# Zero products ahead of the first transposes, a fixed order on three engines, and a first scale column in two parts, in a two-layer trunk on one Trainium2 core

## The chip, the core and the metric

The kernel runs on one core of a Trainium2 chip. Five engines work side by side, each through its own queue in order: TensorE (PE; the profile lists its weight loads apart as PEld) multiplies matrices into PSUM banks, VectorE (DVE) and ScalarE (ACT) do elementwise work and read the banks, GpSimd (POOL) fills tiles and issues some transfers, and SyncE (SP) issues most of the transfers. The metric is the device time of one execution in microseconds, as the median of several runs. Lower is better.

## What is computed

A chunk of 512 tokens of width 1024 goes through two layers. Each layer has a token mixer and a feed-forward part, and each of these is wrapped in the same frame: a norm, a scale and a shift that come from a conditioning vector `c`, the mixer itself, a second norm and a gate. The first mixer is an attention without softmax.

```python
def rms_norm(x, g):
    xf = x.astype(jnp.float32)
    y = xf * lax.rsqrt(jnp.mean(xf * xf, axis=-1, keepdims=True) + EPS)
    return (y * g.astype(jnp.float32)).astype(x.dtype)

def ada_modulation(c, w, b):
    m = jax.nn.silu(c) @ w + b
    shift, scale, gate = jnp.split(m, 3, axis=-1)
    return shift[:, None, :], scale[:, None, :], gate[:, None, :]

def reference(x, c, ...):
    for i in range(DEPTH):
        shift, scale, gate = ada_modulation(c, mix_ada_w[i], mix_ada_b[i])
        h = rms_norm(x, mix_pre_g[i]) * (1.0 + scale) + shift
        if i % N_MIXERS == 0:
            y = stick_breaking_mixer(h, sb_w_qkv[j], sb_w_o[j])
        else:
            y = token_mixing_mixer(h, tm_w_in[j], ...)
        x = x + gate * rms_norm(y, mix_post_g[i])
        ...
        y = swiglu(h, ffn_w_gate[i], ffn_w_up[i], ffn_w_down[i])
        x = x + gate * rms_norm(y, ffn_post_g[i])
    return x
```

This text is about the very beginning: the first `rms_norm`, the first `scale` and `shift`, and the first projection `h @ w_qkv`.

## The kernel before

Tokens are taken in four tiles of 128 (`tt` 0 to 3), the width of 1024 in eight blocks of 128 (`k` 0 to 7). A product of two float32 matrices is made from three products of parts (`mm3`): each operand is split into a high part (ACT, `wh`, `hTh`) and the rest (DVE, `wl`, `hTl`).

The first stage works as follows.

- `norm0(tt)` squares a tile of x on ACT (into `junk`, with the sum in `sx`), takes the root on ACT (`sd`), the reciprocal on DVE (`r`), and scales the tile on DVE.
- `turn0(tt)` turns the tile with eight transposes on PE into two PSUM banks (`tp`). Four copies then bring it into `xhT`, which holds x with the width on the partitions. Before the change ACT makes two of them and DVE two for tiles 0 and 1; ACT makes all four for tiles 2 and 3.
- `row0(raws)` multiplies silu(c), one column (`sc`), with a block of the modulation weights (`ada`): eight products of 1 by 256 in float32, four for each of two weight tiles, into one bank. The result (`row`) is copied by DVE and set upright by two small products with `oneb`. `row0(a0)` gives scale and shift of block k = 0, `row0(a1)` those of k = 1. Those of the other blocks are summed by DVE (`ada0_sum`, with `acc`), set upright by `sums0`, and started by `cols0`.
- `h0` applies scale and shift to a block of `xhT` on ACT, twice: once rounded (`hTh`), once in full; DVE forms the difference `hTl`.
- `v_step` and `qk0_step` multiply block after block with the weights of v (`v`), q (`pq`) and k (`pk`), 512 columns at a time. When all eight blocks are through, the second half of v follows (`v1` in the code), and the attention starts beside it.

Weights come through `wget` and `wemit` in a fixed stream: SP loads a 512 KB tile (`raw`), ACT forms `wh`, DVE forms `wl`. There are two `raw` tiles, so the third load waits until `wl` of the first is made. The weights of the modulation have eight tiles of their own (`ra`) in a pool that is closed after the stage; tiles called `ones`, which POOL fills and SP completes, then take that memory. `G`, the gate of the first mixer, is summed by DVE from `rawada` tiles in eight steps.

The order of each engine's queue is chosen by a scheduler at build time from the code's order and its own estimates. Three switches override it: while `pe["chain"]`, `dve.chain` or `act.chain` is set, each new instruction that goes through the wrapper of that engine is bound to stand behind the last one. Before the change none of them is set in the first stage; PE's is set where the attention starts, so from there PE's queue is written out in the code. `bank` gives PSUM banks in turn: six under one tag, two under the tag "p".

Of the kernel before, what the change touches and what calls it, by code (L numbers as in the profile page):

```python
# [8 lines left out]
F32 = mybir.dt.float32  # L9
F32R = mybir.dt.float32r  # L10
AF = mybir.ActivationFunctionType
ALU = mybir.AluOpType

P = 128
# [21 lines left out]
def trunk(ctx: ExitStack, tc: tile.TileContext, A: dict, out: bass.AP):  # L36
# [17 lines left out]
    def nm(s):  # L54
        uid[0] += 1
        return f"{s}_{uid[0]}"

    def slot(dt, name, a=2, b=512):
        return s4.tile([P, a, b], dt, tag="s4", name=nm(name))

    def bank(name, tag="b"):
        return psum.tile([P, 512], F32, tag=tag, bufs=6 if tag == "b" else 2, name=nm(name))

    pe = {"prev": None, "chain": False}

    class Vector:


        chain, prev = False, None
# [11 lines left out]
    dve = Vector()  # L81

    class Scalar:


        chain, prev = False, None
# [8 lines left out]
    act = Scalar()  # L95

    def pe_op(b):

        if pe["chain"] and pe["prev"] is not None:
            order(b, pe["prev"])  # L100
        pe["prev"] = b

    def order(b, before):
        tc.add_manual_dep(
            b.ins, before.ins.name,
            mybir.DependencyInfo(mybir.DependencyClass.NoSync, mybir.DependencyReason.DATA),
            reason="order",
        )

    def mm(o, l, r, start, stop, after=None):  # L110
        b = nc.tensor.matmul(o, l, r, start=start, stop=stop, skip_group_check=True)  # L111
        pe_op(b)
        if after is not None:
            order(b, after)
# [3 lines left out]
    def transpose(o, i):  # L118
        last_tp[0] = nc.tensor.transpose(o, i, ident)  # L119
        pe_op(last_tp[0])  # L120
# [21 lines left out]
    last_low = [None]  # L142
    last_block, summed, normed = [None], [None], [None]

    raws = []
# [11 lines left out]
    def wemit():  # L157
        n = len(got)
        src, a, b, key = stream[n]
        if len(raws) == n:  # L160
            wload()
        if key[0] == "vblocks":
            got.append(vblocks(raws[n]))
            return
        if src is None:
            if key[1][0] != "u" and (not first_blocks or n > first_blocks[-1] + KF):
                first_blocks.append(n)
            for _ in blocks(*next_raws(n)):
                pass
            return  # L170
        raw = raws[n]
        if key[0] == "wdn" and key[2] in SEVEN[key[1]]:
            got.append(down_blocks(raw))
            return
        h, l = wtile(a, b, SHORT if key[0] in ("wgu", "win_u") else 16)
        if key[0] == "wqk" and key[1]:

            act.activation(h[:], raw[:], AF.Copy)
            nc.vector.tensor_tensor(l[:], raw[:], h[:].bitcast(F32), ALU.subtract)
            if len(raws) == n + 1 and stream[n + 1][3][0] == "wqk":  # L180
                wload()
        else:
            high = act.activation(h[:], raw[:], AF.Copy)
            last_low[0] = nc.vector.tensor_tensor(l[:], raw[:], h[:].bitcast(F32), ALU.subtract)  # L184
            if edge[0] and key[0] == "wgu":
                order(high, feature[1])
                order(last_low[0], feature[0])
        got.append((h, l))
# [154 lines left out]
    def wget(src, look=3):  # L343

        n = taken[0]
        taken[0] += 1
        while len(got) < min(n + 1 + look, len(stream)):
            wemit()
        assert stream[n][3] == src, (stream[n][3], src)
        return got[n]  # L350
# [44 lines left out]
    stp = st0.__enter__()  # L395

    def ada0_raw(b, q):

        nk, n = (4, 256) if b < 2 else (2, 512)
        raw = stp.tile([P, nk, n], F32, tag="ra", bufs=8, name=nm("ada0"))  # L400
        load(raw[:], A["ada0s"][b, q] if b < 2 else A["ada0p"][b - 2, q])
        return raw
# [3 lines left out]
    x0, a0 = [], []  # L406
    for tt in range(NT):
        xt = slot(F32, "x0", 1, 1024)
# [104 lines left out]
    def rms(part, first=None):  # L513

        bias = epsb
        if first is not None:
            bias = small.tile([P, 1], F32, tag="ss", name=nm("ss"))
            dve.tensor_scalar(bias[:], first, 1.0 / D, EPS, ALU.mult, ALU.add)
        sd = small.tile([P, 1], F32, tag="sd", name=nm("sd"))
        last_sqrt[0] = act.activation(sd[:], part, AF.Sqrt, bias=bias[:], scale=1.0 / D)  # L520
        r = small.tile([P, 1], F32, tag="r", name=nm("r"))
        return sd, r
# [201 lines left out]
    def norm0(tt):  # L724
        xt = x0[tt]
        junk = npool.tile([P, D], F32, tag="n", name=nm("junk"))
        sx = small.tile([P, 1], F32, tag="sx", name=nm("sx"))
        act.activation(junk[:], xt, AF.Square, accum_out=sx[:])
        sd, r1 = rms(sx[:])
        dve.reciprocal(r1[:], sd[:])  # L730
        dve.tensor_scalar(xt, xt, r1[:, 0:1], None, ALU.mult)

    def turn0(tt):
        xt = x0[tt]
        for q in range(2):
            ps = bank("tp0")
            for k in range(4):
                kk = q * 4 + k
                transpose(ps[:, k * P : (k + 1) * P], xt[:, kk * P : (kk + 1) * P])
            for k2 in range(2):  # L740
                dst = xhT[q * 2 + k2][:, :, tt * P : (tt + 1) * P]
                src = ps[:, k2 * 256 : (k2 + 1) * 256].rearrange("p (a b) -> p a b", a=2)
                if q and tt < 2:
                    dve.tensor_copy(dst, src)
                else:
                    act.activation(dst, src, AF.Copy)
# [47 lines left out]
    def cols0(k):  # L794

        ps = bank("ab0", "p")
        mm(ps[:, 0:4], ident, add[:, k : k + 2, :].rearrange("p n a -> p (n a)"), True, False)
        return ps
# [8 lines left out]
        )  # L807
        return ab

    def row0(raws):  # L810

        ps = bank("ab0", "p")
        for q, raw in enumerate(raws):
            for k in range(4):
                mm(ps[0:1, :256], sc[:, q * 4 + k : q * 4 + k + 1], raw[:, k, :], q + k == 0, q * 4 + k == 7)
        row = stp.tile([P, 256], F32, tag="row", bufs=2, name=nm("row"))
        dve.tensor_copy(row[0:1, :], ps[0:1, :256])
        ps = bank("ab0", "p")
        for i in range(2):
            mm(ps[:, i : i + 1], row[0:1, i * P : (i + 1) * P], oneb[0:1, 0:1], True, True)  # L820
        return ps
# [16 lines left out]
    wv0, wqk0 = [], []  # L838

    def qk0_step(k):  # L840
        for w, pb in zip(wqk0, (pq0, pk0)):
            h, l = hTk(hT, k, 0, T)
            mm3(pb[:], w[0][:, k, :], w[1][:, k, :], h, l, k == 0, k == KD - 1)

    norm0(0)
    norm0(1)
    turn0(0)
    norm0(2)
    ab0 = row0(a0)
    turn0(1)  # L850
    norm0(3)
    turn0(2)
    turn0(3)
    wv0.append(wget(("wv", 0, 0), 0))
    a2 = [ada0_raw(2, q) for q in range(4)]
    h0(scales(ab0, 0), 0, 0)
    ab1 = row0(a1)
    wqk0.append(wget(("wqk", 0, 0), 0))
    vb = [bank("v0") for _ in range(NT)]
# [6 lines left out]
    for b in range(1, 4):  # L866

        ps = cols0(2 * b)
# [34 lines left out]
    with tc.tile_pool(name="att", bufs=1) as att, tc.tile_pool(name="att2", bufs=2) as att2:  # L903
# [60 lines left out]
        for js in (B31, B2, B0):  # L964
            at, n = {}, 0
# [131 lines left out]
        zb = [bank("z") for _ in range(2)]  # L1097
        bg.bank = lambda: zb[0]
        cur = attend(0)
        for k in range(KD):  # L1100
            if k % 2 == 0:
                wv = wget(("wv", 1, k // 2))
# [7 lines left out]
            if k > 3:  # L1110
                tt = TURNS[k - 4]
# [693 lines left out]
```

## Time and profile before

| what | value |
|---|---|
| median of 3 runs | 1103.92 us (1100.98, 1103.92, 1109.13) |
| the profiled execution's own time | 1103.49 us |
| its span in the profile | 1101.7 us |
| DVE busy, ACT busy, POOL busy over the span | 88%, 55%, 3% |
| bytes read from memory, mean rate | 164.69 MB, 157 GB/s |
| first stage until the first v product | 0 to 22.94 us |
| v, q and k products over all blocks | 22.94 to 61.59 us |

The span is what the profile covers, from the first to the last instruction; the execution's own time has 1.8 us around it. All times below are microseconds from the start of the span. A row of the timeline gives start, duration, engine, line, operation, the tile written and the tiles read, partitions and elements, and how many equal instructions in a row it stands for. In brackets stands how long the engine was idle before, and what ended that.

A float32 product is run as two instructions: `row0` makes eight products, and the timeline counts sixteen. A row's duration on PE contains the time that a product needs to pass through the array, so the starts of successive rows, not their durations, give the pace.

### The profile page before, as it was taken

How to read it: one execution, taken by the hardware profiler on the slowest of the kernel's cores; microseconds unless marked ns; L12 is line 12 of the kernel's file. 1: busy time of each engine (PE TensorE's matmuls, PEld its weight loads, DVE VectorE, ACT ScalarE, POOL GpSimd, SP SyncE). 2: the span in 40 equal slices, each digit the busy share in tenths (PEclk: the TensorE clock that was granted, in tenths of full speed). 3: DMA queues.
4: the chain of work that ended last, by engine and by line, in shares of the span. 5: the costliest groups of instructions: out<-in, count | busy, mean ns of one | idle time of the engine just before them, and what ended most of it. 6: DMA issues, size and time to landing. Idle time of an engine off the chain costs nothing.

```text
span 1101.7 us, 18701 instructions
## 1 busy us (share of the span) xinstructions
PE 1082.1 (98%) x7452; PEld 978.7 (89%) x7452; DVE 972.8 (88%) x1293; ACT 610.1 (55%) x1016; POOL 29.5 (3%) x53
## 2 busy tenths in 40 slices
PE   7999999999999999999999999999999999999997
PEld 4787788788999999998888899988999999999996
DVE  4988999866989999989978999868979999899996
ACT  6554665665655555554252767526545555565662
POOL 0020100000000000001000000001000000000000
PEclk9999999999999999999999999999999999999999
DMA  8976434304433434359878324524334342332252
GB/s 317 357 226 218 138 121 131 122 17 153 153 111 124 163 124 153 134 187 347 294 246 322 143 87 137 177 95 163 122 113 153 136 159 100 107 113 96 77 190 78
DMA packets 51355, 176.38 MB, mean 160 GB/s; under 512 B 6074, under 2 KB 9146, under 8 KB 51268
## 3 DMA queue, kind: packets, MB, share of 16 engines
q1 hardware_dynamic: 48708, 166.81, 43.8%
q0 software_dynamic: 2560, 8.39, 2.1%
q8 instruction: 58, 0.95, 0.3%
q14 instruction: 29, 0.24, 0.1%
HBM read 164.69 MB, written 8.39 MB: 157 GB/s over the span
## 4 chain that ended last, share of the span: by engine, by line
PE 85%; DVE 7%; DMA 4%; issue 2%; ACT 2%; SPq 0%; DVEq 0%; ACTq 0%
PE r L111 35%; PE y L111 16%; PE pqk L111 7%; PE X L111 4%; PE gu L111 4%; PE Y L111 3%; PE v L111 3%; PE u L111 2%; PE av L111 2%; PE z L111 2%; PE tw L119 1%; PE Z L111 1%; PE W L111 1%; PE tp L119 1%; DVE wl L184 1%
## 5 line engine op out<-in xcount | busy, mean ns | idle before, releaser
L111 PE MATMUL r<-Sh,wh 128*128 128x256 f32 x640 | 177.3, 277 | 0.6 <-ACT e L89 0.6
L111 PE MATMUL r<-Sl,wh 128*128 128x256 f32 x640 | 177.0, 277 | 0.0
L111 PE MATMUL r<-Sh,wl 128*128 128x256 f32 x640 | 176.9, 277 | 0.0
L89 ACT ACTIVATE wh<-raw 128x1024 fp32r<-128x1024 f32 (+1 forms) x105 | 108.3, 1036 | 101.7 <-DMA raw<-in_wdown 36.1
L111 PE MATMUL y<-wh,as 128*128 128x512 f32 x480 | 150.5, 391 | 0.3 <-DVE svt L73 0.3
L111 PEld LDWEIGHTS r<-Sh,wh 128*128 128x128 f32 x640 | 120.2, 188 | 1.2 <-ACT e L89 1.0
L111 PEld LDWEIGHTS r<-Sl,wh 128*128 128x128 f32 x640 | 120.2, 188 | 0.1
L111 PEld LDWEIGHTS r<-Sh,wl 128*128 128x128 f32 x640 | 120.1, 188 | 0.0
L184 DVE TENSOR_TENSOR wl<-raw,wh 128x1024 fp32r<-128x1024 f32 x79 | 95.9, 1220 | 25.9 <-ACT wh L89 25.7
L73 DVE TENSOR_TENSOR wl<-f,wh 128x1024 fp32r<-128x1024 f32 x95 | 112.9, 1219 | 1.1 <-ACT wh L89 1.1
L89 ACT ACTIVATE wh<-f 128x1024 fp32r<-128x1024 f32 x95 | 100.2, 1055 | 17.3 <-DVE f L73 12.5
L111 PEld LDWEIGHTS y<-wh,as 128*128 128x128 f32 x480 | 90.0, 188 | 19.3 <-issue 0.6
L89 ACT ACTIVATE e<-r 128x256 f32<-128x256 f32 x120 | 45.9, 384 | 102.3 <-PE r L111 100.2
L111 PE MATMUL y<-wl,as 128*128 128x512 f32 x240 | 93.7, 391 | 0.0
L111 PE MATMUL r<-hTh,wh 128*128 128x256 f32 x320 | 88.8, 278 | 0.2 <-DVE gu L73 0.2
L111 PE MATMUL r<-hTh,wl 128*128 128x256 f32 x320 | 88.5, 277 | 0.0
L111 PE MATMUL r<-hTl,wh 128*128 128x256 f32 x320 | 88.5, 277 | 0.0
L111 PEld LDWEIGHTS r<-hTh,wh 128*128 128x128 f32 x320 | 60.1, 188 | 1.1 <-DVE gu L73 0.9
L111 PE MATMUL r<-hTh,b 128*128 128x256 f32 x320 | 60.9, 277 | 0.0
L111 PEld LDWEIGHTS r<-hTl,wh 128*128 128x128 f32 x320 | 60.1, 188 | 0.0
L111 PEld LDWEIGHTS r<-hTh,wl 128*128 128x128 f32 x320 | 60.1, 188 | 0.0
L89 ACT ACTIVATE wh<-rawx 128x1024 fp32r<-128x1024 f32 x40 | 42.5, 1062 | 29.7 <-PE r L111 28.9
(288 smaller groups left out, 2924.3 us busy)
## 6 DMA issues: line engine op xcount, KB each, us to landing
rawada<-in_ada SPq DMA_DIRECT2D x80, 512.0 KB, 6.3
rawy<-in_wy SPq DMA_DIRECT2D x38, 512.0 KB, 4.2
rawx<-in_wx SPq DMA_DIRECT2D x38, 512.0 KB, 3.4
raw<-in_wdown SPq DMA_DIRECT2D x22, 512.0 KB, 5.3
raw<-in_wdn SPq DMA_DIRECT2D x22, 512.0 KB, 3.4
raw<-in_wqk SPq DMA_DIRECT2D x16, 512.0 KB, 4.0
ada<-in_ada0p SPq DMA_DIRECT2D x12, 512.0 KB, 7.6
raw<-in_wgu SPq DMA_DIRECT2D x12, 512.0 KB, 3.5
```

Source lines behind the costliest of these rows:

```text
L73: b = getattr(nc.vector, op)(*args, **kw)
L89: b = nc.scalar.activation(*args, **kw)
L111: b = nc.tensor.matmul(o, l, r, start=start, stop=stop, skip_group_check=True)
L119: last_tp[0] = nc.tensor.transpose(o, i, ident)
L184: last_low[0] = nc.vector.tensor_tensor(l[:], raw[:], h[:].bitcast(F32), ALU.subtract)
```

## The change

`zero` is a tile of 128 by 256 zeros, filled by DVE, and `spin(n)` lets PE multiply it with itself n times into a bank `zb` that nobody reads. Twenty such products stand ahead of the first transposes, six between those of tile 0 and tile 1. `norm0` is split, so that the root, the reciprocal and the scaling (`root`) can stand behind the copies of an earlier tile. `turn0` takes both banks first and returns the copies as a function; ACT now copies the first bank and DVE the second for every tile. `row0(a0)` makes its first four products, then calls `between`, which holds the transposes and copies of tile 3 and the split of the first weight of v, and then makes the other four. Throughout, the order is bound on PE, DVE and ACT.

```diff
         act.activation(junk[:], xt, AF.Square, accum_out=sx[:])
-        sd, r1 = rms(sx[:])
-        dve.reciprocal(r1[:], sd[:])
-        dve.tensor_scalar(xt, xt, r1[:, 0:1], None, ALU.mult)
+
+        def root():
+            sd, r1 = rms(sx[:])
+            dve.reciprocal(r1[:], sd[:])
+            dve.tensor_scalar(xt, xt, r1[:, 0:1], None, ALU.mult)
+
+        return root
 
     def turn0(tt):
         xt = x0[tt]
+        tps = [bank("tp0") for q in range(2)]
         for q in range(2):
-            ps = bank("tp0")
             for k in range(4):
                 kk = q * 4 + k
-                transpose(ps[:, k * P : (k + 1) * P], xt[:, kk * P : (kk + 1) * P])
+                transpose(tps[q][:, k * P : (k + 1) * P], xt[:, kk * P : (kk + 1) * P])
+        return lambda: copies0(tt, tps)
+
+    def copies0(tt, tps):
+        for q, ps in enumerate(tps):
...
-                if q and tt < 2:
+                if q:
                     dve.tensor_copy(dst, src)
                 else:
                     act.activation(dst, src, AF.Copy)
...
-    def row0(raws):
+    zero = stp.tile([P, 256], F32, name="zero")
+    dve.memset(zero[:], 0.0)
+    zb = bank("zb")
+
+    def spin(n):
+
+        for _ in range(n):
+            mm(zb[:, 0:256], zero[:, 0:P], zero[:], True, True)
+
+    def row0(raws, between=None):
 
         ps = bank("ab0", "p")
         for q, raw in enumerate(raws):
+            if q and between is not None:
+                between()
             for k in range(4):
...
-    norm0(0)
-    norm0(1)
-    turn0(0)
-    norm0(2)
-    ab0 = row0(a0)
-    turn0(1)
-    norm0(3)
-    turn0(2)
-    turn0(3)
-    wv0.append(wget(("wv", 0, 0), 0))
+    pe["chain"] = dve.chain = act.chain = True
+    norm0(0)()
+    root = norm0(1)
+    spin(20)
+    turned = turn0(0)
+    root()
+    spin(6)
+    for tt in (2, 3):
+        root = norm0(tt)
+        turned()
+        turned = turn0(tt - 1)
+        root()
+    turned()
+
+    def between():
+        turn0(3)()
+        wv0.append(wget(("wv", 0, 0), 0))
+        order(last_low[0], dve.prev)
+
+    ab0 = row0(a0, between)
+    pe["chain"] = dve.chain = act.chain = False
```

In the rows of the order below, a name carries a running number, and `x_1` to `x_4` are the token tiles 0 to 3. First PE from its first product to the first v product, before:

```order
L119 MATMUL tp_39_164<-identt,x_1_89 128x128 x4
L119 MATMUL tp_40_171<-identt,x_1_89 128x128 x4
L119 MATMUL tp_48_200<-identt,x_2_95 128x128 x4
L119 MATMUL tp_49_207<-identt,x_2_95 128x128 x4
L111 MATMUL ab_45_186<-ada_5_101,sc 1x256 x4
L111 MATMUL ab_45_186<-ada_6_103,sc 1x256 x4
L119 MATMUL tp_54_222<-identt,x_3_97 128x128 x4
L111 MATMUL ab_47_197<-oneb,row_195 128x1 x2
L119 MATMUL tp_57_243<-identt,x_4_99 128x128 x4
L111 MATMUL ab_65_268<-ada_8_107,sc 1x256 x4
L111 MATMUL v_70_286<-wh_250,hTh_132 128x512
```

The same stretch of PE after the change:

```order
L111 MATMUL zb_150<-zero 128x256 x20
L119 MATMUL tp_38_182<-identt,x_1_89 128x128 x4
L111 MATMUL zb_150<-zero 128x256 x6
L119 MATMUL tp_44_210<-identt,x_2_95 128x128 x4
L119 MATMUL tp_50_232<-identt,x_3_97 128x128 x4
L111 MATMUL ab_54_251<-ada_5_101,sc 1x256 x4
L119 MATMUL tp_55_256<-identt,x_4_99 128x128 x4
L119 MATMUL tp_56_257<-identt,x_4_99 128x128 x4
L111 MATMUL ab_54_251<-ada_6_103,sc 1x256 x4
L111 MATMUL ab_60_280<-oneb,row_278 128x1 x2
L111 MATMUL ab_66_297<-ada_8_107,sc 1x256 x4
L111 MATMUL v_71_315<-wh_270,hTh_132 128x512
```

The zero products stand ahead of the first transposes and again ahead of those of tile 1; the products of the first scale column now end behind the transposes of tile 3, and the two small products (`oneb`) behind them, where before they stood ahead of most of tile 2's and all of tile 3's.

Now DVE, from the scaling of tile 3 (`x_4`) to the first scale and shift (`ab`), before:

```order
L73 TENSOR_SCALAR x_4_99<-x_4_99,r_219 128x1024
L73 COPY row_195<-ab_45_186 1x256
L184 TENSOR_TENSOR wl_251<-raw_105,wh_250 128x1024
L73 TENSOR_TENSOR ab_262<-ab_47_197,add 128x2
L73 TENSOR_TENSOR ab_262<-ab_262,mul 128x2
L73 TENSOR_TENSOR hTl_133<-xhT_128,hTh_132 128x512
L184 TENSOR_TENSOR wl_283<-raw_111,wh_282 128x1024
```

And DVE after the change:

```order
L73 TENSOR_SCALAR x_4_99<-x_4_99,r_244 128x1024
L73 COPY xhT_130<-tp_51_233 128x2x128
L73 COPY xhT_130<-tp_56_257 128x2x128
L184 TENSOR_TENSOR wl_271<-raw_105,wh_270 128x1024
L73 COPY row_278<-ab_54_251 1x256
L184 TENSOR_TENSOR wl_312<-raw_111,wh_311 128x1024
L73 TENSOR_TENSOR ab_291<-ab_60_280,add 128x2
L73 SCALAR_TENSOR_TENSOR acc_347<-ada_61_283,sc,acc_347 128x512
L73 TENSOR_TENSOR ab_291<-ab_291,mul 128x2
```

The copy of `row` moved behind the first `wl`, and the scale and shift moved behind the second `wl` and one step of a sum.

Last SP's queue at the end of the v, q and k products, around the tiles called `ones` and the loads for the gate, before:

```order
L128 DMA G_458<-in_adab 1x1024
L128 DMA cc<-in_consts 128x128
L128 DMA raw_640<-in_wv 128x1024
L128 DMA rawada_527<-in_ada 128x1024
L128 DMA rawada_575<-in_ada 128x1024
L128 DMA ones_607<-in_consts 128x128 x4
L128 DMA raw_646<-in_wv 128x1024
```

And after the change:

```order
L128 DMA cc<-in_consts 128x128
L128 DMA raw_669<-in_wv 128x1024
L128 DMA G_487<-in_adab 1x1024
L128 DMA ones_636<-in_consts 128x128 x3
L128 DMA rawada_556<-in_ada 128x1024
L128 DMA rawada_604<-in_ada 128x1024
L128 DMA raw_675<-in_wv 128x1024
```

Three loads of `ones` now stand ahead of the last five `rawada` loads, where they stood behind them. No queue differs in its order from the middle of the attention on.

## The prediction

> **What bounds the kernel now.** I read the page first, then the windows of the first stage, then its timeline row by row, since the change touches nothing behind it.
>
> ```profile
> PE 1082.1 (98%) x7452; PEld 978.7 (89%) x7452; DVE 972.8 (88%) x1293; ACT 610.1 (55%) x1016; POOL 29.5 (3%) x53
> ...
> PE 85%; DVE 7%; DMA 4%; issue 2%; ACT 2%; SPq 0%; DVEq 0%; ACTq 0%
> ```
>
> PE is busy for 98% of the span and carries 85% of the chain that ended last. So a time that is added to PE in the first stage should reach the end, unless a later wait takes it up. The windows show where that could happen (columns: stretch, length, busy time and count of PE, PEld, DVE, ACT, POOL, granted clock, DMA share, GB/s).
>
> ```profile
> 7.31:12.00 4.69, 3.95 (x17) 3.22 (x18) 2.50 (x6) 4.46 (x12) 0.00 (x0) 1.00 0.98 394
> ...
> 17.00:23.00 6.00, 6.00 (x37) 3.36 (x36) 2.48 (x6) 4.87 (x11) 0.00 (x0) 1.00 0.99 405
> 23.00:60.00 37.00, 36.38 (x172) 29.42 (x172) 35.64 (x48) 16.95 (x23) 4.84 (x10) 1.00 0.81 300
> ```
>
> From 23 to 60 us PE is busy for 36.38 of 37.00 us and DVE for 35.64: both are nearly full. The granted clock is 1.00 in each window, but the pace of the products is not the same, as the timeline of the start shows:
>
> ```profile
> 0.90 0.07 DVE L73 MEMSET mul<- 128x8 f32 x1
> ...
> 6.50 0.75 DVE L73 TENSOR_SCALAR x<-x,r 128x1024 f32<-128x1024 f32 x1
> ...
> 7.31 1.97 PE L119 MATMUL tp<-identt,x 128*128 128x128 f32 x8 [7.31 <-DVE x L73]
> ...
> 10.02 1.97 PE L119 MATMUL tp<-identt,x 128*128 128x128 f32 x8 [0.74 <-DVE x L73]
> ...
> 11.92 4.96 PE L111 MATMUL ab<-ada,sc 128*1 128x256 f32 x16
> ...
> 12.30 0.12 PEld L111 LDWEIGHTS ab<-ada,sc 128*1 128x1 f32 x1 [0.30 <-issue]
> ...
> 13.87 1.06 ACT L89 ACTIVATE wh<-raw 128x1024 fp32r<-128x1024 f32 x1
> ...
> 14.43 0.13 PEld L111 LDWEIGHTS ab<-ada,sc 128*1 128x1 f32 x1 [0.30 <-issue]
> 14.78 1.59 PEld L111 LDWEIGHTS ab<-ada,sc 128*1 128x1 f32 x8 [0.22 <-issue]
> ...
> 16.92 0.41 DVE L73 COPY row<-ab 1x256 f32<-1x256 f32 x1 [3.28 <-PE ab L111]
> 17.26 1.20 DVE L184 TENSOR_TENSOR wl<-raw,wh 128x1024 fp32r<-128x1024 f32 x1
> 17.51 0.66 ACT L89 ACTIVATE xhT<-tp 128x256 f32<-128x256 f32 x2 [2.59 <-PE tp L119]
> ...
> 17.51 0.60 PE L111 MATMUL ab<-oneb,row 1*128 1x1 f32 x4
> ...
> 18.05 1.42 PE L119 MATMUL tp<-identt,x 128*128 128x128 f32 x11
> ...
> 18.49 0.33 SPq L128 DMA_DIRECT2D raw<-in_wqk  x1
> ...
> 19.39 3.61 PE L111 MATMUL ab<-ada,sc 128*1 128x256 f32 x16
> 20.23 0.85 ACT L89 ACTIVATE hTh<-xhT,ab 128x512 fp32r<-128x512 f32 x1
> ...
> 22.94 0.50 PE L111 MATMUL v<-wh,hTh 128*128 128x512 f32 x1
> ```
>
> PE idles until tile 0 is scaled and starts at 7.31. The weight loads of `row0` stand 0.426 us apart from 12.30 to 14.43 (five steps), then eight stand in 1.59 us, about 0.21 apart. A transpose takes 1.97/8 = 0.246 us before 12 us and 1.42/11 = 0.129 us after 18 us. So PE runs at half pace until about 14.6 us. From 10.02 to 22.94 it has next to no gap: the first v product waits for PE's own queue.
>
> **The zero products.** One float32 product is two instructions here (eight products, x16). The twenty are 40 instructions of 256 columns. At half pace each takes 0.426 us. At full pace the nearest row is a v product, whose weight load has the same 128 columns and whose pace comes from the next fence: 15 starts from 38.22 to 41.39, so 3.17/14 = 0.2264 us.
>
> ```profile
> 24.38 0.73 DVE L73 SCALAR_TENSOR_TENSOR acc<-ada,sc,acc 128x512 f32<-128x512 f32 x1
> ...
> 24.98 0.60 PE L111 MATMUL ab<-oneb,row 1*128 1x1 f32 x4
> ...
> 26.55 0.28 PE L111 MATMUL ab<-add,identt 128*128 128x4 f32 x2
> ...
> 38.22 0.39 PE L111 MATMUL v<-wh,hTh 128*128 128x512 f32 x1
> ...
> 41.39 0.39 PE L111 MATMUL pq<-hTh,wl 128*128 128x512 f32 x1
> ...
> 50.26 0.95 PE L111 MATMUL ab<-oneb,acc 128*128 128x1 f32 x8
> ...
> 61.59 0.39 PE L111 MATMUL v<-wh,hTh 128*128 128x512 f32 x1
> ```
>
> They can start when DVE has filled `zero`, behind the fill that ends at 0.97. No row shows that fill; I take 0.3, for a start at 1.3. How long the half pace lasts is the open term. Before, it ended 2.7 us after the first product of `row0` (11.92) or 7.3 us after the first transpose. I take 4 us, nearer to the row with like products: 4/0.426 = 9.4 instructions at half pace, 30.6 x 0.2264 = 6.9 us for the rest, so the twenty end at 1.3 + 4 + 6.9 = 12.2. Call that moment E. The bounds: full pace from the first instruction gives 1.3 + 40 x 0.2264 = 10.4; half pace for 7.3 us gives 1.3 + 7.3 + 22.9 x 0.2264 = 13.8. In each case tile 0, ready at 7.25, waits for PE. The first transposes start 12.2 - 7.31 = 4.9 us later (bounds 3.1 and 6.5).
>
> [...]
>
> **From E to the first v product.** PE, at full pace: transposes of tile 0, 8 x 0.129 = 1.03; six zero products, 12 x 0.2264 = 2.72; tiles 1 and 2, 2.06 (DVE scales tile 2, 0.75, behind two copies of tile 0, in time, while the zeros run); four products of `row0`, half of 3.55 (16 in the row at 19.39 until 22.94), 1.78; tile 3, 1.03; four more, 1.78. PE is through at E + 10.40. But `row` must be copied by DVE, and that copy now stands behind `wl`. Tile 3's transposes end at E + 8.62; ACT copies 0.66, forms `wh` in 1.06, DVE forms `wl` in 1.20 and copies `row` in 0.41: with a few hundredths for each handover E + 12.1. So PE waits 1.7 us here, a stall that is new. Then the small products, 0.60 with a handover, until E + 12.8, and `row0(a1)`, 3.55: the first v product at E + 16.35. The other way to it is shorter: a second `wl` of 1.20 behind `row`, one `acc` step of 0.73 between two short ones for `ab`, then `hTh`, 0.85 on ACT: about E + 15.2.
>
> Before, the same stretch took 22.94 - 7.31 = 15.63 us. So full pace saves there (transposes of tiles 0 and 1 1.9 us, `row0` 1.4, the gap ahead of 10.02 0.74), and the six zero products (2.7) and the new stall (1.7) cost a little more: +0.7 us.
>
> **Behind it.** Two rows of the page's list of loads (issues, size, median us to landing) are needed here and for the first rival:
>
> ```profile
> rawada<-in_ada SPq DMA_DIRECT2D x80, 512.0 KB, 6.3
> ...
> raw<-in_wqk SPq DMA_DIRECT2D x16, 512.0 KB, 4.0
> ```
>
> From 22.94 to 61.59, 38.65 us, PE makes 144 products of 0.2264, 32.6 us, and small ones: 0.60, three of 0.28, three of about 0.95, together 4.3. So 1.75 us were waits, the most that a better order could give back. DVE comes to the v products with one `wl` and one `acc` step already made, and ACT with one `wh`; I take 0.6 us back, and nothing or all of it as bounds. Splitting copies alike between ACT and DVE and taking the second bank early I cost at nothing: the copies hide behind zero products and `row0` at E + 1 to E + 7.5, and only tile 3's, counted above, do not. SP's first 13 loads do not move. The third load, into a `raw` tile that `wl` frees, goes out with that `wl`, at E + 11.7, 23.9 against 18.49 before; with the median of 4.0 us it lands at 27.9, ahead of the first v product.
>
> **The sum.** 4.9 + 0.7 - 0.6 = +5.0 us on PE, which carries the chain to the end: 1103.49 (the profiled execution's own time) becomes 1108.5. The median of the runs stands 0.43 above that execution, so I predict 1108.9. With the bounds: 3.1 + 0.7 - 1.75 = +2.0, and 6.5 + 0.7 = +7.2, so 1106.0 to 1111.1.
>
> **Rivals.** First: a later stall on top. Loads for the gate now stand behind three `ones` loads, and DVE, in order, makes the five gate steps ahead of the second `wl` of `v1`.
>
> ```profile
> 42.88 4.25 SPq L128 DMA_DIRECT2D rawada<-in_ada  x5
> ...
> 46.92 3.11 DVE L73 SCALAR_TENSOR_TENSOR acc<-ada,sc,acc 128x512 f32<-128x512 f32 x4
> ...
> 54.63 1.85 POOL L974 MEMSET ones<- 128x1027 f32 x2 [20.40 <-DMA rawada<-in_ada]
> ...
> 55.62 2.70 SPq L128 DMA_DIRECT2D ones<-in_consts  x6
> ...
> 57.41 6.56 DVE L73 SCALAR_TENSOR_TENSOR G<-rawada,sc,G 128x1024 f32<-128x1024 f32 x5
> ...
> 65.62 2.36 DVE L184 TENSOR_TENSOR wl<-raw,wh 128x1024 fp32r<-128x1024 f32 x2 [0.46 <-ACT wh L89]
> ...
> 67.03 0.39 PE L111 MATMUL v<-wh,hTh 128*128 128x512 f32 x1
> ```
>
> The memory for `ones` comes free behind the last sum, 50.03 + 5.0 = 55.0 at the earliest. SP's loads follow 1.0 later; three take 1.35 and the five gate loads 4.25: 61.6. At the median of 6.3 us the last lands at 67.9, its step of 1.31 ends at 69.2, and `wl` is 2.83 us behind, as it was (66.80 behind 63.97): 72.0. PE needs it at 67.03 + 5.0 = 72.0. So a landing slower than 6.3 us decides it; at 9 us PE waits 2.7 us and the time is 1111.6. For it: it is a tie. Against it: fewer loads compete there, since the gate loads are what competed before.
>
> Second, on the other side of no change: the zeros hide in PE's first idle time, if each were one instruction and not two. 9.4 at half pace and 10.6 x 0.2264 give E = 7.7, the six cost 1.36 less, v starts at 22.7, and with 0.6 back the time is 1103.9 - 0.9 = 1103.0, not slower. It decides from E below 8.6, where E - 7.31 + 0.7 - 1.36 - 0.6 is nothing. Against it stands the x16 for eight products.
>
> Third: the change does not do what it says, and zeros leave the half pace. Then E = 1.3 + 40 x 0.426 = 18.3; transposes of three tiles take 5.9 in place of 3.1, the six zeros 5.1 in place of 2.7, and `row0`'s first half about 3.0 in place of 1.8, so the shift is 11.0 + 6.4 + 0.7 - 0.6 = 17.5, and the time 1121.4, 1.6% slower. What speaks for it: no row here has zeros. [...]
>
> **How the numbers follow.** My forecast (+2 to +7) has 0.72; the later stall 0.13; the hidden zeros 0.07; zeros that do not raise the pace 0.05; 0.03 is left for a gain or loss that I do not see. The range has to hold the forecast and the later stall and the scatter of the runs (1100.98 to 1109.13): 1103 to 1113. One per cent, 11 us, is about what a measurement of this kernel can tell from no change. Only the third rival and a share of the rest lie beyond it: slower 0.06, faster 0.01, same 0.93. Within that, I expect slower.
>
> **What the profile after would show.** A row of zero products x40 from about 1.3 to 12.2, with a change of pace near 5; the first transposes x8 in 1.03 us, not 1.97; `row0(a0)` in two rows, paced 0.22; an idle time of PE of about 1.7 us put down to DVE `row`; the first v product near 28.5; the first product of `v1` near 66.6. Wrong would be: a v product before 25, a half pace beyond 9 us, or a shift at `v1` that is gone at the end.

## The result, and the profile after

The changed kernel takes 1111.82 us (median of six runs, 1111.48 to 1116.15), the kernel before 1103.07 us beside it (six runs, 1100.98 to 1109.13). The ratio is 1.0081, with a 95% interval of 1.0062 to 1.0099: slower by 0.8%, and less than the one per cent that was called a change. The profiled execution took 1111.73 us, its span is 1110.0 us.

The page says little: PE is busy for 98% of the span as before, and carries 88% of the chain that ended last.

```profile
PE 1093.1 (98%) x7504; PEld 988.4 (89%) x7504; DVE 973.2 (88%) x1298; ACT 609.2 (55%) x1012; POOL 29.5 (3%) x53
...
PE 88%; DVE 5%; DMA 3%; issue 1%; ACT 1%; SPq 0%; POOL 0%; DVEq 0%; ACTq 0%; POOLq 0%
```

The timeline of the start, in the columns of the rows shown in the prediction:

```profile
0.98 0.27 DVE L73 MEMSET zero<- 128x256 f32 x1
...
1.30 10.51 PE L111 MATMUL zb<-zero 128*128 128x256 f32 x40 [1.30 <-DVE zero L73]
...
11.65 1.04 PE L119 MATMUL tp<-identt,x 128*128 128x128 f32 x8
...
12.52 2.76 PE L111 MATMUL zb<-zero 128*128 128x256 f32 x12
...
15.12 1.91 PE L119 MATMUL tp<-identt,x 128*128 128x128 f32 x16
...
18.77 1.09 PE L119 MATMUL tp<-identt,x 128*128 128x128 f32 x8
...
19.46 0.66 ACT L89 ACTIVATE xhT<-tp 128x256 f32<-128x256 f32 x2 [0.91 <-PE tp L119]
20.01 2.00 ACT L89 ACTIVATE wh<-raw 128x1024 fp32r<-128x1024 f32 x2
...
21.10 1.23 DVE L184 TENSOR_TENSOR wl<-raw,wh 128x1024 fp32r<-128x1024 f32 x1 [0.44 <-ACT wh L89]
22.24 0.40 DVE L73 COPY row<-ab 1x256 f32<-1x256 f32 x1
...
22.70 0.60 PE L111 MATMUL ab<-oneb,row 1*128 1x1 f32 x4 [1.02 <-DVE row L73]
...
26.77 0.50 PE L111 MATMUL v<-wh,hTh 128*128 128x512 f32 x1
...
64.93 0.39 PE L111 MATMUL v<-wh,hTh 128*128 128x512 f32 x1
```

The zero products do what was said of them. They are two instructions each (x40); the starts stand 0.426 us apart at first and 0.216 apart from about 4.5 on; the eight transposes behind them take 1.04 us and not 1.97. They also keep tile 0, which is scaled at 7.5, waiting until 11.65. The first v product comes 3.83 us later than before (22.94), the first product of `v1` 3.34 us later (61.59).

The span is 8.3 us longer, though, and so 4.9 us are lost behind `v1`. Comparing the starts of like PE instructions in the two traces, the shift is still 3.34 at 90 us, then 6.76 at 110 and 8.23 at the end. Of the last 1.5 us, 0.5 come near 325 us, where PE waits 1.11 us for ACT (0.59 before); the rest comes behind 600 us, in steps of the size by which single executions differ there (run 12 below: 1.2 us). The larger place is in this timeline of PE and DVE, in the attention's first part:

```profile
95.98 1.23 DVE L179 TENSOR_TENSOR wl<-raw,wh 128x1024 fp32r<-128x1024 f32 x1 [1.57 <-ACT wh L89]
97.12 2.29 DVE L73 TENSOR_TENSOR_SCAN left<-ga,ones 128x1025 f32<-128x1025 f32 x1
...
97.54 0.44 PE L111 MATMUL av<-acch,ones 128*128 128x512 f32 x1
...
99.32 0.67 DVE L73 TENSOR_TENSOR G<-av,g 128x512 f32<-128x512 f32 x1
99.90 0.68 DVE L73 TENSOR_TENSOR accl<-G,acch 128x512 fp32r<-128x512 f32 x1
...
100.64 0.80 PE L111 MATMUL av<-accl,ones 128*128 128x512 f32 x1 [2.66 <-DVE accl L73]
101.23 0.63 PE L111 MATMUL pqk<-hTh,wh 128*128 128x512 f32 x1
101.66 0.63 PE L111 MATMUL pqk<-hTl,wh 128*128 128x512 f32 x1
...
103.70 0.39 PE L111 MATMUL pqk<-hTh,wh 128*128 128x512 f32 x1
103.93 0.40 PE L111 MATMUL pqk<-hTl,wh 128*128 128x512 f32 x1
```

Two products with `ones` spread the gate's second half, `acch` and `accl`, over all rows. DVE makes `accl` behind a weight's `wl`, a scan of 2.29 us and the first half of the gate. PE, whose order is written out there, waits 2.66 us. Before, the same wait was there and shorter, and DVE itself had waited for the load of `g`:

```profile
93.97 0.69 DVE L73 TENSOR_TENSOR G<-av,g 128x512 f32<-128x512 f32 x1 [0.82 <-DMA g<-in_post_g]
...
95.31 0.50 PE L111 MATMUL av<-accl,ones 128*128 128x512 f32 x1 [1.10 <-DVE accl L73]
```

In the changed kernel the products then start 0.43 us apart (101.23, 101.66) until 103.4, and 0.23 apart from 103.70: between two starts lay 3.10 us (1.49 before), and PE fell back to half its pace for the `accl` product and six more, some 1.4 us on top.

Why is DVE late? Here are the windows from 60 to 75 us of the kernel before (columns as in the prediction), then rows of the changed kernel's timeline, of SP, ACT and DVE, then its windows:

```profile
60.00:65.00 5.00, 5.00 (x24) 4.14 (x23) 4.89 (x6) 3.14 (x6) 4.30 (x8) 1.00 0.99 345
65.00:70.00 5.00, 5.00 (x24) 4.14 (x23) 3.61 (x4) 1.54 (x2) 0.43 (x1) 1.00 0.93 271
70.00:75.00 5.00, 5.00 (x30) 3.83 (x29) 2.56 (x4) 2.69 (x4) 0.00 (x0) 1.00 0.88 290
```

```profile
55.25 2.60 SPq L128 DMA_DIRECT2D rawada<-in_ada  x5
...
69.08 0.33 SPq L128 DMA_DIRECT2D raw<-in_wv  x1
...
76.39 1.06 ACT L89 ACTIVATE wh<-raw 128x1024 fp32r<-128x1024 f32 x1 [7.58 <-DMA raw<-in_wv]
...
77.48 1.23 DVE L184 TENSOR_TENSOR wl<-raw,wh 128x1024 fp32r<-128x1024 f32 x1 [7.30 <-ACT wh L89]
```

```profile
60.00:65.00 5.00, 5.00 (x24) 4.14 (x23) 4.86 (x5) 2.95 (x5) 0.99 (x2) 1.00 1.04 400
65.00:70.00 5.00, 5.00 (x24) 4.14 (x23) 4.55 (x5) 3.25 (x5) 3.72 (x7) 1.00 1.01 355
70.00:75.00 5.00, 5.00 (x24) 4.14 (x23) 0.18 (x1) 0.00 (x0) 0.00 (x0) 1.00 1.04 284
```

The five gate loads, issued at 42.88 before, go out at 55.25. From 60 to 75 us the DMA engines are full (share 1.01 to 1.04), the last weight of `v1` needs 7.3 us from its issue at 69.08 to ACT's `wh` (before, 3.9 us from 66.88 to the row below), and DVE stands idle for 7.30 us: busy for 0.18 of the 5 us from 70 on, where it was 2.56. PE feels nothing of it until its written order comes to `accl`, 25 us later. ACT's row of the kernel before:

```profile
70.77 1.06 ACT L89 ACTIVATE wh<-raw 128x1024 fp32r<-128x1024 f32 x1 [4.22 <-DMA raw<-in_wv]
```

There is a second move in SP's queue, of which the forecast did not speak. The fourth load for A (`rawada_947` below) waits for a tile that DVE must free, and what stands behind it waits too. Before, it stood behind the q/k weight that follows it here (`raw_880`). SP's queue after the change:

```
L128 DMA raw_777<-in_wqk 128x1024
L128 DMA raw_826<-in_wqk 128x1024
L128 DMA rawada_947<-in_ada 128x1024
L128 DMA raw_880<-in_wqk 128x1024
L128 DMA g_888<-in_post_g 128x1024
```

### The profile page after: what moved, and what is told of

Same layout as the page of the kernel before. It is cut to its first block, busy times and chain, and to the rows that moved or that the text cites. A ratio compares the mean times of both kernels' runs of the same rounds, so it can differ in the third digit from the quotient of the medians.

```text
span 1110.0 us, 18801 instructions
## 1 busy us (share of the span) xinstructions
PE 1093.1 (98%) x7504; PEld 988.4 (89%) x7504; DVE 973.2 (88%) x1298; ACT 609.2 (55%) x1012; POOL 29.5 (3%) x53
## 4 chain that ended last, share of the span: by engine, by line
PE 88%; DVE 5%; DMA 3%; issue 1%; ACT 1%; SPq 0%; POOL 0%; DVEq 0%; ACTq 0%; POOLq 0%
PE r L111 35%; PE y L111 16%; PE pqk L111 7%; PE gu L111 6%; PE X L111 4%; PE Y L111 3%; PE v L111 3%; PE u L111 2%; PE av L111 2%; PE z L111 2%; PE tw L119 1%; PE Z L111 1%; PE W L111 1%; PE tp L119 1%; PE zb L111 1%
```

## Experiments

Theory: the zeros delay PE by two to three microseconds, and the rest is the order of the loads, which the scheduler chose anew from its estimates, and which makes `accl` late. Rivals: the zeros cost everything; the written order on DVE and ACT does; or the place of one load does. All kernels compute everything; the zero products are read by nobody.

**1. No zeros.** `spin(20)` and `spin(6)` become `spin(0)`.

> The changed kernel without its 26 zero products; the written order and the split scale column stay. The gate's last five loads stand ahead of the ones loads again, as before the change. Theory (two parts: a later start, then late gate loads): the first transposes start near 7.5 at half pace, the wait for row behind the first wl stays, the first v product comes near 25.2 (before 22.94, changed 26.77), the first product of v1 near 63.2, there is no wait of PE for accl above 1.5 us, and the time is 1104 to 1106. Rival (the zero products win back what they cost, the written order is what costs): v near 27 or later and 1110 or more.

Measured: 1107.07 us (1105.05 to 1109.32), ratio to the kernel before 1.0026 [1.0015, 1.0037]. v started at 24.37, `v1` at 62.87, as expected, but the time lies above the expected 1104 to 1106: the shift of 1.28 us at `v1` was 4.48 at 110 us. The wait at `accl` was there without a single zero product:

```profile
98.09 0.50 PE L111 MATMUL av<-accl,ones 128*128 128x512 f32 x1 [2.60 <-DVE accl L73]
```

In this kernel the gate loads were back ahead of `ones`, but the fourth load for A still stood ahead of a q/k weight. So the rest of the change, without zeros, leads to that second move. The time of this run therefore doesn't tell what the written order costs by itself.

**2. Gate loads held ahead.** The changed kernel, and:

```diff
-                        load(raw, A["ada"][s, part, j % KD])
+                        last_gate[0] = load(raw, A["ada"][s, part, j % KD])
...
-                load(t[:, o : o + P], A["consts"][:, 1, :])
+                order(load(t[:, o : o + P], A["consts"][:, 1, :]), last_gate[0])
```

> The changed kernel with one bond more: the ones loads stand behind the gate's eight loads in SP's queue, as before the change. Theory (two parts): the first v product stays at 26.8 and the first product of v1 at 64.9, but the wait of PE for accl near 97.5 (2.66 us) and the half pace behind it go, so 3 to 4 us of the 8.8 are gone: 1107 to 1109. Rival (the later start alone makes the later collision, whatever the order of the loads): the wait stays and the time is 1111 to 1112.

Measured: 1108.34 us (1107.86 to 1108.77), 1.0039 [1.0024, 1.0054], as expected. v at 26.83 and `v1` at 64.96 are those of the changed kernel. The second `accl` product came at 98.11, the same time as without zeros (98.09), though PE was 2 us later up to there: `accl` has its own time, set by the loads and by DVE, and PE takes the later of the two.

**3. Zeros alone.** The kernel before, plus `zero`, `spin(20)` and `spin(6)`, bound on PE only.

> The kernel before with the 26 zero products alone, bound on PE ahead of and behind the transposes of tile 0; no order is written on DVE and ACT, copies and the scale column are as before. The scheduler then puts row0 ahead of tile 1's transposes, and the gate's last five loads behind three ones loads, as in the changed kernel. Theory (two parts): zeros from 1.3 to 11.6, the first v product between 25.5 and 27, and the late gate loads cost 2 to 3.5 us near 95: 1108 to 1111. Rival (the written order is what costs): 1103 to 1105.

Measured: 1114.55 us (1114.18 to 1114.79), 1.0091 [1.0076, 1.0106]: slower than expected, and than the whole change. `v1` came at 64.79, only 3.2 us late; the two `accl` products then waited (idle 2.43 and 2.66 us), with 2.8 and 3.2 us between starts, and the shift was 9.5 at 110 us. Here too the scheduler had put the gate loads behind `ones`.

**4. No zeros, `row` copied early.** No zero products, and the copy of `row` ahead of the first `wl`.

> The changed kernel without zero products and with the copy of row ahead of the first wl on DVE. Here the scheduler puts the gate's last five loads behind three ones loads without any zero product. Theory (two parts): the first v product near 23.5 to 24.5, the first product of v1 near 62, yet PE waits for accl near 95 for 2 us or more, and the time is 1105 to 1108, above that without zeros and with the early loads less the 1 to 1.5 us that the copy gives. Rival (the later start alone makes the later collision): no wait above 1.5 us and 1102 to 1104.

Measured: 1113.48 us (1112.53 to 1114.84), 1.0083 [1.0064, 1.0102], where 1105 to 1108 was expected. v came at 23.45, early; but this small edit made the scheduler put the gate loads behind `ones`, and a weight of `v1` behind both (issued at 59.52; in the changed kernel at 42.87). Now PE waited for that weight, 4.24 us:

```profile
67.71 0.49 PE L111 MATMUL v<-wh,hTh 128*128 128x512 f32 x1 [4.24 <-ACT wh L89]
```

About fifteen products at half pace followed (0.43 us apart until 75.1), so the shift went from 1.72 at 60 us to 10.18 at 80. Without any zero product the late loads cost as much as the whole change. Next, the order of the loads by itself.

**5. Both bonds.** As run 2, and the fourth load for A behind the weight loads:

```diff
-        load(raw[:], src)
+        raw_loads.append(load(raw[:], src))
...
+                        if name == "A" and at == 0 and j == 3:
+                            order(last_gate[0], raw_loads[-2])
```

> The changed kernel with two bonds on SP's queue and nothing else changed: the loads of ones stand behind all eight gate loads (as in the run with the tail held), and the fourth load for A, which waits for DVE, stands behind the q/k weight loads that it held up. Theory (the second part of the loss is the order of the loads): first v product still near 26.8, v1 still near 65.0, no wait of PE over 1.5 us at the two accl products, so the shift stays near +3.4 us to the end: 1107.0 us (1106.2 to 1107.8). Rival (the place of A's fourth load is worth nothing): as with the tail held alone, 1108.3 us, and accl still near 98.1. Second rival (zeros make the whole loss): 1111 or more.

Measured: 1107.34 us (1105.65 to 1107.76), 1.0032 [1.0018, 1.0047]. The wait is gone, as expected:

```profile
96.98 0.40 PE L111 MATMUL av<-acch,ones 128*128 128x512 f32 x1
97.22 0.39 PE L111 MATMUL av<-accl,ones 128*128 128x512 f32 x1
```

But the shift did not stay: 3.16 at 90 us became 1.81 at 110, since the wait that the kernel before has there no longer follows. The profiled execution took 1105.65 us and is the fastest of the five. The second bond also puts A's fourth load behind `g` and one weight more, a little later in the queue than the kernel before has it.

**6. A's load alone.** The changed kernel with the second bond only.

> The changed kernel with one of the two bonds alone: the fourth load for A behind the q/k weight loads that it held up; the gate loads stay behind the loads of ones. With it the four cases are complete (changed kernel 1111.8 us, gate loads held 1108.3, both 1107.3). Theory (the late gate loads fill the DMA engines and make DVE late from 65 us on; the place of A's load adds only DVE's idle time of 1.6 us ahead of the scan): v near 26.8, v1 near 64.9, accl near 99, still a wait of PE of over 1 us there, 1110.0 us (1109.0 to 1111.3). Rival (A's load alone makes the loss): accl near 96.5, no wait, 1107.3 us.

Measured: 1111.32 us (1109.96 to 1113.0), 1.0076 [1.0059, 1.0093]; `accl` at 100.08, with a wait of 2.29 us. It gave half a microsecond where 1.8 was expected. With runs 2 and 5 the four cases are: neither bond 1111.8, A's load 1111.3, gate loads 1108.3, both 1107.3 us. The bond on the gate loads is worth the larger part; what the bond on A's load gives here lies within the intervals. So A's load alone doesn't make the loss. And since all four have the zeros, these aren't the whole of it, so the first rival falls.

**7. No zeros, A's load held.** Run 1 with the second bond.

> The changed kernel without its zero products, and with the fourth load for A behind the q/k weight loads that it held up. Theory: without zeros PE starts v at 24.4 and v1 at 62.9 (1.3 behind the kernel before), and accl, which came at 98.1 without this bond, comes near 95.5, so the shift stays near 1.3 and the time falls from 1107.1 to 1105.2 us (1104.4 to 1106.0). Rival: accl is late for another reason (DVE's written order); then it stays at 98 and the time at 1107.

Measured: 1104.44 us (1103.2 to 1107.76), 1.0010 [0.9999, 1.0021]. Against run 1 the bond gives 2.6 us by the medians and 0.16% (1.8 us) by the ratios. Run 5, which has the zeros besides (and the first bond, without which they would move the gate loads), is 2.9 us slower by the medians and 0.22% by the ratios (the two intervals just overlap): the price of the zeros with loads in order.

**8. Zeros alone, both bonds.** Run 3 with them.

> The kernel before plus the zero products (20 and 6) only, as in the run with zeros alone (1114.6 us), but with the two bonds on SP's queue. Theory (zeros cost their delay of 3.2 us at v1, and the rest of the 10.7 us came from the loads that the scheduler moved): v near 27.1, v1 near 64.8, no wait over 1.5 us at the accl products, 1107.2 us (1106.4 to 1108.4). Rival (zeros cost all of it): still above 1112.

Measured: 1105.52 us (1104.26 to 1106.15), 1.0012 [0.9999, 1.0024], 1.7 us better than expected, and 9 us better than run 3. v (26.74) and `v1` (64.44) were as late as there. So the same zeros cost 0.1% or 0.9%, depending on the order in which SP issues its loads.

**9. No zeros, `row` early, both bonds.** Run 4 with them.

> The run without zeros and with the copy of row ahead of the first wl (1113.5 us, v1 at 67.7 behind a wait for its weight), now with the two bonds on SP's queue. No zero product in either. Theory (all that was lost there came from the gate loads that the scheduler put behind the loads of ones): v stays near 23.5, the wait of 4.6 us ahead of v1 is gone and v1 near 62.0, accl near 95.5, 1104.3 us (1103.4 to 1105.4). Rival (the written order of DVE and ACT loses it): v1 still near 67, above 1110.

Measured: 1105.59 us (1104.62 to 1108.27), 1.0014 [1.0004, 1.0024], against 1113.48 in run 4 and a little above what was expected. The bond also brings the weight of `v1` forward again (issued at 42.74). `v1` came at 63.65 where 62.0 was expected, since from v (23.80) to there PE needed 39.85 us and not 38.65; among its waits is one of 0.5 us for a `wl` of k's weights that the kernel before does not have. It looks as if an earlier v only meets its weights sooner; where the rest of the 1.2 us went was not traced.

**10. Ten zeros.** Ten ahead of tile 0, none ahead of tile 1, `row` early, A's load held; meant to beat the kernel before.

> The changed kernel with ten zero products ahead of tile 0 and none ahead of tile 1, the copy of row ahead of the first wl, and the fourth load for A behind the q/k weight loads. Theory: ten products (eight instructions at 0.426, twelve at 0.216, from 1.3) end at 7.3, when tile 0 is ready, and leave PE at full pace there: transposes of tile 0 at 0.13 each, first v product near 21.8 (1.1 ahead of the kernel before), v1 near 60.5, loads in the order of before, end 1102.3 us (1101.3 to 1103.5), a little faster than before. Rival: PE has gaps between tile 0 and tile 2 without the six zeros, falls back to half pace, v near 23.5 and the time 1104 to 1106.

Measured: 1108.34 us (1104.9 to 1109.01), 1.0033 [1.0015, 1.0051]; no gain. The twenty instructions ended late, since the half pace lasted longer here:

```profile
1.30 7.51 PE L111 MATMUL zb<-zero 128*128 128x256 f32 x20 [1.30 <-DVE zero L73]
8.66 1.04 PE L119 MATMUL tp<-identt,x 128*128 128x128 f32 x8
```

v still came at 22.69, 0.25 earlier than before, and at 110 us the shift was 0.01: the start of v is not what bounds. The profiled execution (1109.0 us; two of the five took 1104.9 and 1105.9) then lost 4.5 us between 290 and 325 us, far from the edit, in the same form as at `accl`. A row of its PE timeline, and a window of it:

```profile
320.01 0.39 PE L111 MATMUL r<-Sh,wh 128*128 128x256 f32 x1 [2.31 <-ACT e L89]
```

```profile
320.00:325.00 5.00, 4.99 (x29) 4.99 (x30) 0.84 (x2) 1.36 (x3) 0.00 (x0) 0.66 0.00 0
```

A wait of 2.31 us, and then a granted clock of 0.66. Why the wait was longer there than in other kernels (0.5 us in run 5) was not followed up.

**11. The changed kernel, scan moved.** The loads stay late; the work that stands ahead of `accl` on DVE is moved behind it:

```diff
-        cur[0](B0)
-        for n in FIRST:
-            fill(n, (2, 6))
+        fill(FIRST[0], (2, 6))
+        cur[0](B0)
+        fill(FIRST[1], (2, 6))
```

> The changed kernel, its loads left as late as they are, with the same move of the scores and the scan behind the second pair of accl products. Theory (DVE's chain of wl, scan, G and accl is what PE waits for near 97.5, and the wait of 3.1 us between two starts also costs the full pace): without the scan ahead of it accl is ready near 98.2, PE reaches it near 96.9, waits 1.0 to 1.8 us and keeps its pace: 1109.3 us (1108.3 to 1110.5) in place of 1111.8. Rival (the late loads take the same time at a later place): 1111 or more.

Measured: 1109.07 us (1108.24 to 1110.74), 1.0048 [1.0033, 1.0064], as expected. PE waits less, 1.18 us at the first pair (94.55) and 0.67 at the second, and keeps its pace:

```profile
98.70 0.50 PE L111 MATMUL av<-accl,ones 128*128 128x512 f32 x1 [0.67 <-DVE accl L73]
```

```profile
100.00:105.00 5.00, 5.00 (x25) 3.86 (x26) 4.46 (x5) 2.74 (x5) 0.00 (x0) 1.00 0.38 133
```

In the changed kernel this window has a granted clock of 0.66.

**12. The kernel before, scan moved.** The same move without the change, and A's fourth load behind `g` and one weight more, so that `g` comes in time.

> The kernel before, with nothing of the change, but with the first scores, sigmoids and scan of the last attention blocks (z, left, 128x1025) moved behind the second pair of accl products, and the fourth load for A behind the load of g and one more q/k weight. Theory (the loads and DVE set when accl is ready near 95 us, and PE in the kernel before already waits 1.1 us for it): accl is ready near 92.5, PE reaches it near 93.1 and does not wait, the shift against the kernel before is -1.0 to -1.4 us from there to the end, 1102.9 us where the kernel before has 1104.0 (ratio 0.9985 to 0.9995). Rival: the scan, now 5 us later, or A's load makes PE wait later instead: no gain, ratio 1.000 to 1.002.

Measured: 1103.65 us (1102.01 to 1104.97, eleven runs) against 1104.53 for the kernel before beside it (1103.51 to 1108.48), ratio 0.9988 [0.9979, 0.9998]: a little faster than the kernel before, within the expected range of ratios; the interval ends just below one. Two things were moved, and their shares were not separated. The wait is gone:

```profile
92.00 0.68 DVE L73 TENSOR_TENSOR accl<-G,acch 128x512 fp32r<-128x512 f32 x1
...
93.40 0.39 PE L111 MATMUL av<-accl,ones 128*128 128x512 f32 x1
```

The shift is -0.87 from 110 to 250 us, though this execution came to `v1` 0.47 us late. Later it drifts to +0.48, where nothing differs between the kernels; a drift of that size is scatter of single executions.

## Why the prediction was right, and where it was not

The forecast was 1108.9 us in a range of 1103 to 1113; 1111.82 lies in it, and so does the 0.8% in "within 1%, and slower". The mechanism at the start was right. What came behind it was forecast wrongly, and two errors partly cancelled.

- **The zeros.** E was put at 12.2; it was 11.65. The half pace lasted about 3.2 us and not 4, and the full pace was 0.216 us and not 0.2264, which was that of products of 512 columns. Shift of the first transposes: +4.3 in place of +4.9.
- **From E to the first v product.** 16.35 us forecast, 15.12 measured. Most of it is the stall for `row`: 1.0 us, not 1.7, since ACT copies tile 3's first bank (19.46) while its second is still being turned, and `wh` begins at 20.01. PE's own work was 0.4 us shorter, since transposes start 0.109 us apart and not the 0.129 that was taken from their durations, and zeros 0.216 and not 0.2264. So the stretch is 0.5 us shorter than before (15.63), not 0.7 longer.
- **Given back up to `v1`.** 38.16 us against 38.65, 0.5 (0.6 forecast). Together +3.34 at `v1`, not +5.0.
- **"+5.0 us on PE, which carries the chain to the end".** This step failed. PE is busy for 98% of the span, but at `accl` it waits for DVE, and DVE's time there comes from the loads. Where loads were in order, the delay was partly swallowed by the wait that the kernel before has (runs 5 and 8: 3.16 to 1.81, 2.85 to 1.51). Where a load was late, `accl` set the time, and PE's delay up to there did not matter (runs 1 and 2, 98.09 and 98.11).
- **The first rival** named the right cause, the gate loads behind `ones`, and by its sum 1111.6 us. Its place was wrong: PE did not wait for `wl` of `v1` (no wait from 65 to 90 us). The wait came at `accl`, and of its price of 3.4 us some 1.4 were the lost pace, which no term had. That the number fits is chance. PE did wait at `v1` in run 4, where a weight of `v1` itself was issued late.
- **The second and third rivals** fell by the first rows: x40, and a pace that doubled.
- **SP's second move**, the fourth load for A, was not seen in the forecast. It costs 1.8 to 2.6 us without zeros (runs 1 and 7); the 0.5 to 1.0 us with them can't be told from nothing.

What the change costs, then: of 0.81%, the order of the loads makes 0.49% (run 5 has 0.32%), the zeros 0.22% (run 5 against run 7; 0.12% in run 8, where they stand alone), and the written order with loads held 0.10% (run 7). The intervals of runs 7 and 8 touch zero, so the last two shares are only roughly known, and the bonds don't restore the order of the kernel before in every place. What stays open: the first bond also moved a weight of `v1` ahead of the gate loads, and the two were not separated. And that the scheduler turned the order of the loads is shown, by zeros (run 3) as by another edit (run 4); why its estimates tip there was not looked into.

## What to carry to other kernels

A busy share of 98% does not make an engine the bound at each place (here PE waited 2.66 us at `accl`): before a delay is added through to the end, look for the next instruction at which that engine waits for another, and ask what sets that other one's time. Where a scheduler orders the queues, an edit at one end can reorder the loads at the other; compare the DMA queue's whole order, and bind what must not move. A wait on PE can cost more than itself when the pace falls behind it (2.66 us here, and some 1.4 us on top), so it can pay to move work from ahead of the awaited result to behind it (run 11: 1109.07 us in place of 1111.82).

## What the runs showed of the hardware

The full pace did not come at a fixed time. The same forty zero instructions took 10.29 (run 6), 10.33 (run 5), 10.51 (the changed kernel), 11.50 (run 8) and 11.86 us (run 3). By the starts of the single instructions, the pace changed 2.6 us after the first in run 6, 3.2 us after it in the changed kernel and 6.0 us after it in run 3: it moves by 3.4 us. What sets the moment was not shown. So, as far as these runs go, a fixed number of zeros can't be fitted to a start time: ten were meant for the shorter case, and run 10, where twenty instructions took 7.51 us, met the longer.

In run 1 the pace rose while PE had nothing but transposes. These are the first rows of PE in run 1 and in run 7; up to 14 us it had nothing but transposes (of run 7 the second row is shown):

```profile
7.36 1.97 PE L119 MATMUL tp<-identt,x 128*128 128x128 f32 x8 [7.36 <-DVE x L73]
11.18 3.44 PE L119 MATMUL tp<-identt,x 128*128 128x128 f32 x16 [1.86 <-DVE x L73]
```

```profile
10.38 3.73 PE L119 MATMUL tp<-identt,x 128*128 128x128 f32 x16 [1.05 <-DVE x L73]
```

The sixteen took 3.73 us in run 7, where all stand 0.213 us apart, and 3.44 us in run 1, where the last start 0.11 us apart, from 14.2 us on. So in run 1 nothing but float32 transposes stood ahead of the change. The pace that the zeros bring comes without them too, some microseconds later: at 14.2 us in run 1 and at 14.7 in the kernel before, against 4.5 in the changed kernel.

Behind a wait of 2.3 to 2.7 us the pace was lost in four kernels, but the length alone doesn't decide. Half pace followed at once on waits of 2.29 (run 6) and 2.66 us (the changed kernel), and 1.3 to 1.5 us behind waits of 2.31 (run 10) and 2.60 us (run 1). It did not follow this wait of run 3, behind which twelve products start 0.23 us apart:

```profile
96.64 0.50 PE L111 MATMUL av<-accl,ones 128*128 128x512 f32 x1 [2.43 <-DVE accl L73]
```

Nor did it follow waits of 1.10 (the kernel before) and 0.67 us (run 11).
